# A row softmax whose tile context is closed behind the first six loads

## The chip, the cores and the metric

The kernel runs on one core of a Trainium2 chip. The metric is the device time of one execution in microseconds. A profile is one further execution, taken by the hardware profiler; its span runs from the first to the last instruction of the program, and the execution's device time is a little longer than that.

A core has several engines with instruction queues of their own: PE (matrix products, without arithmetic here), DVE (vector work), ACT (functions of one argument), POOL (a further vector engine) and SP, which only issues copies and waits. Sixteen copy engines, called DMA in the profile, move the data between device memory and on-chip memory.

## The reference

```python
def setup_inputs():
    batch, seq, dim = 16, 1024, 512
    return {
        "x": np.random.randn(batch, seq, dim).astype(np.float32),
    }

def reference(x: np.ndarray) -> np.ndarray:
    x_max = np.max(x, axis=-1, keepdims=True)
    exp_x = np.exp(x - x_max)
    return (exp_x / np.sum(exp_x, axis=-1, keepdims=True)).astype(np.float32)
```

A softmax over each of 16384 rows of 512 values: 33.55 MB in, 33.55 MB out, in float32.

## The kernel before

**Tiles and stages.** The rows are cut into 16 groups of 128 partitions by 8 rows (`GROUP`); one group is 128 x 4096 values, 2 MB. A load or a store moves two groups, 4 MB, so there are eight of each, called L0 to L7 and S0 to S7 here. The on-chip buffer `ring` holds 12 groups, that is six loads; everything is computed in place in it. L6 and L7 reuse the places of the first four groups, so they have to wait until S0 and S1 have read them out (`before` maps each late load to its store, `awaited` lists these stores).

**One group.** DVE takes the negated row maxima into `stat` (`rowmax`, line 146); ACT computes the exponential of each row with this as bias and leaves the row's sum in the same place (`exps`, line 135, a loop on ACT alone with eight row operations in an iteration); DVE inverts the sums into `recip` (line 160); and DVE or POOL multiplies the group by them (`scale`, line 162).

**What sets the order.** Three lists written by hand. `SEQUENCE` is the order of the work on DVE and POOL: M or MM is a maximum over one or two groups, D a scaling on DVE, P one on POOL. `ORDER` is the order of SP's late transfers. `AT_HEAD` says how many loads are lifted, after the program has been traced, out of the body's first block and put ahead of the barrier that opens the program (`loads_at_the_head`): one, on SP. The engines wait for each other through semaphores of the kernel's own: `loaded` for each load, `maxima`, `summed`, `inverted`, `scaled` for each store, and `stored` for the two stores that late loads wait for. The other stores raise `others`.

**What the tile context does.** The whole kernel is traced inside a tile context, a layer that finds dependences, adds its own semaphores and orders instructions. Six loads, a fence and the load of ACT's function table stand in a region with the order as written; `no_tile_sem_insts` lists the loads as copies that carry no semaphore of the context. All computation and the late transfers up to S6 stand in a critical section (line 186), which the context takes as one unit: on entry and on exit the engines of the section meet, here by way of PE. The last store, S7, follows the section, and behind it SP waits for `others` (line 207). On leaving the context (line 233, in the launch code) it adds an end of its own: a wait for what it tracks, a drain of every engine, a barrier, a clear of its semaphores by POOL, and a second barrier. Line 222 is the program's own opening, with a barrier too.

Of the kernel before, what the change touches and what calls it, by code (L numbers as in the profile page):

```python
# [8 lines left out]
EXP = mybir.ActivationFunctionType.Exp  # L9
AX = mybir.AxisListType.X  # L10
ACT, DVE, POOL, PE, SP = [
    getattr(mybir.EngineType, e) for e in ("Activation", "DVE", "Pool", "PE", "SP")
]
# [7 lines left out]
STORES = [2, 2, 2, 2, 2, 2, 2, 2]  # L21
# [1 line left out]
LOAD_AT = [sum(LOADS[:k]) for k in range(len(LOADS))]  # L23
STORE_AT = [sum(STORES[:k]) for k in range(len(STORES))]


ORDER = """
S0 S1 L6 L7 S2 S3 S4 S5 S6
"""


SEQUENCE = """
# [28 lines left out]
@with_exitstack  # L61
def kernel(
    ctx: ExitStack,
    tc: tile.TileContext,
    x: bass.AP,
    out: bass.AP,
):
    nc = tc.nc
    nc.at_finalize(loads_at_the_head)
    P = nc.NUM_PARTITIONS  # L70

    x_rows, out_rows = x.flatten_outer_dims(), out.flatten_outer_dims()
    d = x_rows.shape[1]
    assert x_rows.shape[0] == P * GROUPS * GROUP

    def sbuf(name, n):
        return ctx.enter_context(nc.sbuf_tensor(name, [P, n], F32))

    ring = sbuf("ring", RING * GROUP * d)

    stat = sbuf("stat", RING * GROUP)
    recip = sbuf("recip", RING * GROUP)

    def sem(name):
        return ctx.enter_context(nc.semaphore(name))

    maxima, summed, inverted = [sem(s) for s in ("maxima", "summed", "inverted")]
    loaded = [sem(f"loaded{k}") for k in range(len(LOADS))]
    scaled = [sem(f"scaled{k}") for k in range(len(STORES))]

    def load_of(g):
        return max(k for k in range(len(LOADS)) if LOAD_AT[k] <= g)

    def store_of(g):
        return max(k for k in range(len(STORES)) if STORE_AT[k] <= g)


    before = {
        k: store_of(LOAD_AT[k] + LOADS[k] - 1 - RING)
        for k in range(len(LOADS))  # L100
        if LOAD_AT[k] >= RING
    }

    awaited = sorted(set(before.values()))
    stored = {k: sem(f"stored{k}") for k in awaited}
    others = sem("others")

    def at(g):
        return g % RING

    def rows(g, groups=1):
        part = ring[:, at(g) * GROUP * d : (at(g) + groups) * GROUP * d]
        return part.rearrange("p (r d) -> p r d", d=d)

    def cols(t, g, groups=1):
        return t[:, at(g) * GROUP : (at(g) + groups) * GROUP]

    def in_dram(t, g, groups):
        k = load_of(g)
        assert load_of(g + groups - 1) == k  # L120
        part = t[P * GROUP * LOAD_AT[k] : P * GROUP * (LOAD_AT[k] + LOADS[k]), :]
        first = (g - LOAD_AT[k]) * GROUP
        part = part.rearrange("(p r) d -> p r d", p=P)
        return part[:, first : first + groups * GROUP, :]

    def load(k):
        g, n = LOAD_AT[k], LOADS[k]
        return nc.sync.dma_start(out=rows(g, n), in_=in_dram(x_rows, g, n))

    def store(k):  # L130
        g, n = STORE_AT[k], STORES[k]
        return nc.sync.dma_start(out=in_dram(out_rows, g, n), in_=rows(g, n))

    def exp(row, one):
        return nc.scalar.activation(  # L135
            out=row, in_=row, func=EXP, bias=one, scale=1.0, accum_out=one
        )

    def spread(t):
        return t.unsqueeze(2).to_broadcast([P, GROUP, d])  # L140


    def rowmax(g, groups):
        assert load_of(g) == load_of(g + groups - 1)
        nc.vector.wait_ge(loaded[load_of(g)], 16)  # L145
        nc.vector.reduce_max(  # L146
            out=cols(stat, g, groups), in_=rows(g, groups), axis=AX, negate=True
        ).then_inc(maxima, groups)

    def exps():  # L150
        with nc.Fori(0, GROUPS, 1, engines=(ACT,)) as g:
            nc.scalar.wait_ge(maxima, 1).then_inc(maxima, -1)  # L152
            row = nc.scalar.snap((g % RING) * GROUP)
            for r in range(GROUP):
                done = exp(ring[:, bass.ds((row + r) * d, d)], stat[:, bass.ds(row + r, 1)])
            done.then_inc(summed, 1)

    def scale(g, engine):
        nc.vector.wait_ge(summed, g + 1)
        nc.vector.reciprocal(out=cols(recip, g), in_=cols(stat, g)).then_inc(inverted, 1)  # L160
        engine.wait_ge(inverted, g + 1)
        engine.tensor_mul(  # L162
            out=rows(g), in0=rows(g), in1=spread(cols(recip, g))
        ).then_inc(scaled[store_of(g)], 1)

    def done_by(k):
        later = [a for a in awaited if a >= k]
        return stored[later[0]] if later else others

    def store_scaled(k):  # L170
        nc.sync.wait_ge(scaled[k], STORES[k])
        store(k).then_inc(done_by(k), 16)

    with tc.manual_schedule(engines={ACT, DVE, POOL, SP}):
        nc.scalar.preload_act_table(EXP)  # L175


        for k in range(min(before)):
            first = load(k).then_inc(loaded[k], 16)
            tc.info.no_tile_sem_insts.add(first.ins.name)  # L180
            tc.add_to_no_dep_group("loads", first.ins)
        tc.declare_fence(nc.sync.nop().ins, group="loads")

        pending = 16 * (len(STORES) - 2 - max(awaited))
        nc.scalar.nop().then_inc(others, pending)
        with tc.tile_critical(sync_engine=PE):
            nc.tensor.wait_ge(others, pending).then_inc(others, -pending)
            exps()
            for work in SEQUENCE.split():
                kind = work.rstrip("0123456789")  # L190
                g = int(work[len(kind) :])
                if kind in ("M", "MM"):
                    rowmax(g, len(kind))
                else:
                    scale(g, nc.vector if kind == "D" else nc.gpsimd)
            for transfer in ORDER.split():
                k = int(transfer[1:])
                if transfer[0] == "S":
                    store_scaled(k)
                else:  # L200
                    last = before[k]
                    since = max([a for a in awaited if a < last], default=-1)
                    nc.sync.wait_ge(stored[last], 16 * (last - since))
                    load(k).then_inc(loaded[k], 16)
            nc.sync.wait_ge(scaled[-1], STORES[-1])
        store(len(STORES) - 1)
        nc.sync.wait_ge(others, pending)


# [28 lines left out]
```

## Time and profile before

| what | value |
|---|---|
| device time, median of three runs | 161.18 us (160.99 to 161.60) |
| device time of the profiled execution | 161.16 us |
| span of the profiled execution | 159.4 us |
| copied | 33.55 MB read, 33.55 MB written |
| mean rate over the span | 421 GB/s |

The costliest groups of instructions; each row has line, engine and operation, what is written from what, and the number; then the busy time in us and the mean of one in ns; then the idle time of the engine just ahead of them and what ended it:

```profile
L135 ACT ACTIVATE ring<-ring,stat x128 | 90.4, 707 | 31.1 <-ACTq L152 31.1
L146 DVE TENSOR_REDUCE stat<-ring 128x16 f32<-128x8192 f32 (+1 forms) x10 | 69.5, 6956 | 15.5 <-DMA ring<-in_x_dram 15.5
L162 POOL TENSOR_TENSOR ring<-ring,recip 128x4096 f32<-128x4096 f32 x6 | 42.1, 7017 | 81.7 <-DVE recip L160 81.7
L162 DVE TENSOR_TENSOR ring<-ring,recip 128x4096 f32<-128x4096 f32 x10 | 51.1, 5110 | 0.3
```

An engine's letter with a q (SPq, POOLq) is its instruction queue: waits, drains, branches and issues of copies, which are not counted as busy.

### The profile page before, as it was taken

The page shows a single profiled execution, that of the slowest core. Times are in us where ns is not written, and L with a number is a line of the kernel's source. Part 1 is how long each engine was busy: PE and PEld are TensorE (multiplying, and loading weights), DVE is VectorE, ACT ScalarE, POOL GpSimd, SP SyncE. Part 2 cuts the span into 40 slices and gives each one's busy share as a digit, 9 for nine tenths or more (in the row PEclk, how much of TensorE's full clock was granted, in tenths as well). Part 3 has the DMA queues.
Part 4 walks back from the last instruction along what each step waited for, and adds up shares of the span by engine and source line. Part 5 has one row for each costly group of instructions (what it writes and reads, how often), then busy time and mean ns, then how long its engine had stood idle before and what let it go on. Part 6 is the DMA issues. An engine that isn't in the chain of part 4 may idle for free.

```text
span 159.4 us, 601 instructions
## 1 busy us (share of the span) xinstructions
DVE 121.8 (76%) x36; ACT 92.3 (58%) x257; POOL 42.3 (27%) x10
## 2 busy tenths in 40 slices
DVE  0009979999999999999999499999999999500000
ACT  3000799969307999999979990998699100000000
POOL 0000000000007904921960890098059100000000
DMA  7999999999999999999999999999999999999993
GB/s 263 444 469 403 428 469 419 395 469 452 395 428 477 411 395 395 395 493 428 395 436 477 403 395 493 428 395 469 436 411 411 477 428 395 477 428 411 436 461 156
DMA packets 2304, 67.11 MB, mean 421 GB/s; under 512 B 256, under 2 KB 256, under 8 KB 256
## 3 DMA queue, kind: packets, MB, share of 16 engines
q1 hardware_dynamic: 2304, 67.11, 98.4%
HBM read 33.55 MB, written 33.55 MB: 421 GB/s over the span
## 4 chain that ended last, share of the span: by engine, by line
DMA 45%; DVE 39%; issue 2%; DVEq 0%
DMA ring<-in_x_dram 25%; DVE ring L162 22%; DMA out_dram<-ring 20%; DVE stat L146 16%; DVE recip L160 1%; DVEq L145 0%
## 5 line engine op out<-in xcount | busy, mean ns | idle before, releaser
L135 ACT ACTIVATE ring<-ring,stat x128 | 90.4, 707 | 31.1 <-ACTq L152 31.1
L146 DVE TENSOR_REDUCE stat<-ring 128x16 f32<-128x8192 f32 (+1 forms) x10 | 69.5, 6956 | 15.5 <-DMA ring<-in_x_dram 15.5
L162 POOL TENSOR_TENSOR ring<-ring,recip 128x4096 f32<-128x4096 f32 x6 | 42.1, 7017 | 81.7 <-DVE recip L160 81.7
L162 DVE TENSOR_TENSOR ring<-ring,recip 128x4096 f32<-128x4096 f32 x10 | 51.1, 5110 | 0.3
L135 ACT ACTIVATION_READ_ACCUMULATOR ring<-ring,stat x128 | 23.8, 186 | 0.0
L160 DVE RECIPROCAL recip<-stat 128x8 f32<-128x8 f32 x16 | 3.0, 191 | 0.0
L175 ACT ACT_TABLE_LOAD x1 | 1.3, 1283 | 0.8 <-PEq L222 0.8
L222 POOL MEMSET const-float32-0.0<- 128x1 f32 x1 | 0.1, 98 | 0.2 <-issue 0.2
L222 POOL MEMSET const-bfloat16-1.0<- 128x1 bf16 x1 | 0.1, 103 | 0.0
L222 POOL MEMSET const-uint8-127<- 128x1 uint8 x1 | 0.1, 103 | 0.0
L222 POOL MEMSET const-float32-1.0<- 128x1 f32 x1 | 0.1, 99 | 0.0
## 6 DMA issues: line engine op xcount, KB each, us to landing
ring<-in_x_dram SPq DMA_DIRECT2D x8, 4096.0 KB, 25.9
out_dram<-ring SPq DMA_DIRECT2D x8, 4096.0 KB, 23.9
```

What stands on the lines that cost most here:

```text
L135: return nc.scalar.activation(out=row, in_=row, func=EXP, bias=one, scale=1.0, accum_out=one)
L146: nc.vector.reduce_max(out=cols(stat, g, groups), in_=rows(g, groups), axis=AX, negate=True).then_inc(maxima, groups)
L160: nc.vector.reciprocal(out=cols(recip, g), in_=cols(stat, g)).then_inc(inverted, 1)
L162: engine.tensor_mul(out=rows(g), in0=rows(g), in1=spread(cols(recip, g))).then_inc(scaled[store_of(g)], 1)
L175: nc.scalar.preload_act_table(EXP)
L222: nc = _bacc.Bacc("TRN2", target_bir_lowering=False, num_devices=1)
```

## The change

The context now holds only the first six loads. It is closed and compiled inside the kernel, and everything else is traced after that, outside any context. The group and the fence of the loads, the preset of `others` and the critical section are gone; the order as written is asked for SP alone, since only SP has instructions inside. S7 joins `ORDER` and raises `others` as the stores from S2 on do; SP's last wait counts six stores instead of five, and a nop follows it. The load of ACT's table follows the close. `SEQUENCE`, the late loads and their waits are the same. `tc.close()` ends the trace of the context and `tc.compile()` turns it into instructions, its end with drains, barriers and the clear among them; leaving the context in the launch code then adds nothing more.

```diff
 ORDER = """
-S0 S1 L6 L7 S2 S3 S4 S5 S6
+S0 S1 L6 L7 S2 S3 S4 S5 S6 S7
 """
...
-    with tc.manual_schedule(engines={ACT, DVE, POOL, SP}):
-        nc.scalar.preload_act_table(EXP)
...
+    with tc.manual_schedule(engines={SP}):
         for k in range(min(before)):
             first = load(k).then_inc(loaded[k], 16)
             tc.info.no_tile_sem_insts.add(first.ins.name)
-            tc.add_to_no_dep_group("loads", first.ins)
-        tc.declare_fence(nc.sync.nop().ins, group="loads")
-
-        pending = 16 * (len(STORES) - 2 - max(awaited))
-        nc.scalar.nop().then_inc(others, pending)
-        with tc.tile_critical(sync_engine=PE):
-            nc.tensor.wait_ge(others, pending).then_inc(others, -pending)
-            exps()
...
-            nc.sync.wait_ge(scaled[-1], STORES[-1])
-        store(len(STORES) - 1)
-        nc.sync.wait_ge(others, pending)
+    tc.close()
+    tc.compile()
+
+    nc.scalar.preload_act_table(EXP)
+    exps()
+    for work in SEQUENCE.split():
...
+    for transfer in ORDER.split():
+        k = int(transfer[1:])
+        if transfer[0] == "S":
+            store_scaled(k)
+        else:
+            last = before[k]
+            since = max([a for a in awaited if a < last], default=-1)
+            nc.sync.wait_ge(stored[last], 16 * (last - since))
+            load(k).then_inc(loaded[k], 16)
+    nc.sync.wait_ge(others, 16 * (len(STORES) - 1 - max(awaited)))
+    nc.sync.nop()
```

More of the change, by code (lines that the diff above doesn't have):

```diff
@@ L180 @@
             tc.info.no_tile_sem_insts.add(first.ins.name)
-            tc.add_to_no_dep_group("loads", first.ins)
-        tc.declare_fence(nc.sync.nop().ins, group="loads")
-        pending = 16 * (len(STORES) - 2 - max(awaited))
-        nc.scalar.nop().then_inc(others, pending)
-        with tc.tile_critical(sync_engine=PE):
-            nc.tensor.wait_ge(others, pending).then_inc(others, -pending)
-            exps()
[L189 to L204, printed above, removed]
-            nc.sync.wait_ge(scaled[-1], STORES[-1])
-        store(len(STORES) - 1)
-        nc.sync.wait_ge(others, pending)
+    tc.close()
[3 more added lines that the diff above has]
+    for work in SEQUENCE.split():
+        kind = work.rstrip("0123456789")
+        g = int(work[len(kind) :])
+        if kind in ("M", "MM"):
+            rowmax(g, len(kind))
+        else:
+            scale(g, nc.vector if kind == "D" else nc.gpsimd)
+    for transfer in ORDER.split():
+        k = int(transfer[1:])
+        if transfer[0] == "S":
+            store_scaled(k)
+        else:
+            last = before[k]
[4 more added lines that the diff above has]
+    nc.sync.nop()
 _INS = ['x']
```

## The prediction

> **What bounds the kernel now.** I read the page first, then the copy queues, the chain of waits, the rows of the opening and of the closing stage, and last the records of semaphore changes, which the trace keeps beside the rows that are printed.
>
> ```profile
> span 159.4 us, 601 instructions
> DVE 121.8 (76%) x36; ACT 92.3 (58%) x257; POOL 42.3 (27%) x10
> DMA  7999999999999999999999999999999999999993
> q1 hardware_dynamic: 2304, 67.11, 98.4%
> ```
>
> No engine fills the span, but the sixteen copy engines do: 98.4% of it, and nine tenths or more in every slice but the first and the last. 67.11 MB is the input once and the output once, so nothing can be left out of it. The chain of waits names DVE for 39%, yet that is only one of two parallel stories: the transfers stand back to back whatever DVE does. Landing times show it. The first load lands at 12.30 us, then 21.98, 31.70, 41.41, 51.12 and 61.35, then S0 at 71.09, S1 at 80.96, L6 at 90.45, L7 at 100.21, and at the end S6 at 148.90 and S7 at 158.57: always 9.5 to 10.2 us, the time of 4 MB. Work is queued well before its turn: S1 is issued at 61.75 against 71.09, S6 at 128.55 and S7 at 138.03 against 148.90. So compute has at least 9.3 us of slack. What can be won lies ahead of the first packet or behind the last.
>
> ```profile
> core 0: us, DVE busy (x) ACT busy (x) POOL busy (x), PEclk, DMA share, GB/s
> 149.00:157.30 8.30, 0.00 (x0) 0.00 (x0) 0.00 (x0) 1.00 0.98 422
> 157.30:158.60 1.30, 0.00 (x0) 0.00 (x0) 0.00 (x0) 1.00 0.01 0
> 158.60:159.40 0.80, 0.00 (x0) 0.00 (x0) 0.00 (x0) 1.00 0.00 0
> ```
>
> The table by stretches shows the end: data moves until 157.3, the completion marks arrive until 158.57, and then 0.8 us pass in which nothing is copied or computed. The rows of line 233 say what these are:
>
> ```profile
> L233 SPq DRAIN  x3: 7/7/7, 158.7 to 159.0; - x3
> L233 POOLq DRAIN  x2: 34/52/71, 158.9 to 159.1; - x2
> L233 POOLq EVENT_SEMAPHORE_RANGE_CLEAR  x1: 73/73/73, 159.0 to 159.0; - x1
> ```
>
> SP's wait for S7 runs from 158.59 to 158.62. Then come a drain on every engine, a barrier (over at about 158.93), POOL's clear of the context's semaphores at 159.01, and a second barrier that PE leaves last, at 159.378, the span's end. The durations are tens of nanoseconds; the hops between engines make the 0.76 us.
>
> **The change part by part.** *The end.* The context's closing moves from behind S7 to behind the first six loads. SP now ends with its wait for the six late stores and a nop. The wait ends at 158.62 as before; for the nop I allow 0.03 (the fence nop of before took 17 ns, and SP starts consecutive instructions about 0.06 apart). The program ends at 158.65 instead of 159.378: 0.73 us less of span.
>
> *Behind the span.* The profiled execution has 161.16 us, 1.78 more than its span. The semaphore records show what happens there: nine increments of semaphore 2 (159.611, .645, .852, .896, .919, 160.017, .057, .091, .138), then all semaphores cleared in five blocks up to 160.699, then nine more increments (160.924 to 161.281). Nine over five engines is a walk there and back. I read the order from the blocks: the lowest (up to 53) clears slowest, 7 ns each, and fits PE, whose semaphore rows take 51 ns against 17 to 21 elsewhere; the highest (207 to 255) starts first, 0.12 us after the fifth increment. That fits SP as the turning point. Before, all engines enter this walk together, PE's first increment is 0.233 after its last instruction, and the third hop, POOL's, takes 0.207 where the second walk needs 0.038: it was late by 0.17. After the change PE is done at about 4 us, POOL at about 124 and DVE at 137.7, so four hops have been walked long before, and only SP is late. Its own way from last instruction to increment isn't shown: at most 159.919 - 159.332 = 0.587, at least nothing, and PE's 0.233 is the nearest row; I take 0.23. The fifth increment then comes at 158.65 + 0.23 = 158.88 instead of 159.919, which is 1.04 us earlier, and all that follows it moves along. With 0.587 the gain is 0.68, with zero 1.27.
>
> The Trainium skill, "Runtime: NRT & Kernel Launch", section "The ~15µs preamble/postamble breakdown", gives such a walk as about 355 ns and lists the runtime's closing stages as fixed lengths added to a kernel. The second walk here agrees (161.281 - 160.924 = 0.357); the first takes 0.527. Taken as fixed lengths, the page speaks against any gain beyond the span, and the sum would be 160.43; by the records it is 160.12.
>
> *The opening.* Behind the sixth load's issue (over at 3.16) SP now passes a drain, two barriers and POOL's clear. The same steps took 0.76 at the end, so the close is over at about 4.0. A drain doesn't wait for copies that are under way: SP's took 7 ns at 137.84 with S5 and S6 queued, and 131 ns at 0.43 behind the first load. Nothing waits for SP then: its next issue is S0 at 39.92.
>
> ```profile
> 0.00 3.16 SPq L128 DMA_DIRECT2D ring<-in_x_dram  x6
> 0.79 1.28 ACT L175 ACT_TABLE_LOAD   x1 [0.79 <-PEq L222]
> 12.32 4.42 DVE L146 TENSOR_REDUCE stat<-ring 128x8 f32<-128x4096 f32 x1 [12.32 <-DMA ring<-in_x_dram]
> ```
>
> The table load moves from 0.79 to about 4.0 and ends near 5.3; ACT first needs it at 17.09. DVE's first reduction waits for the load until 12.32 in any case. Cover for all of this: 8.3 us. If that were gone, the price would still be nothing until 9.3 us more are lost.
>
> *The critical section.* The fence nop, ACT's preset of `others`, PE's wait, and the section's exit go. The exit held S7 from 137.69 to 138.03, so S7 is issued 0.34 earlier. S6 occupies the copy engines until 148.90, so this is worth nothing. SP's waits, the late loads and their order stay, on the same queue. The loads lose their group and fence; since they write different parts of the ring and carry no semaphore of the context, none is held behind another.
>
> *Sum.* 161.16 - 1.04 = 160.12 us. The profiled execution lies 0.02 below the median of the runs, 161.18, so this is 0.66% under that median.
>
> **The rivals.** *Only the program's own tail goes.* The runtime keeps its 1.78 us behind the program. For it: the walk can start with something that counts from the last engine's end, and SP's way into it may be as long as the bound of 0.587. Against it: POOL's late hop shows that the walk waits for arrivals. 161.16 - 0.73 = 160.43, which is 0.46% under the median.
>
> *The close waits for the six loads* (slower). A context that ends could wait for all that it issued. Place: the drain at 3.2 us, on every engine. For it: at the end of before, the context does wait for S7 (158.59). Against: that store carries the context's own semaphore 127; the six loads are excepted from these. Price: compute starts at 61.35 + 0.8 = 62.2 instead of 12.32. DVE needs 137.66 - 12.32 less 3.2 of later load waits, 122.1, so S7 is issued at 184.3; S6, 9.5 ahead, lands some 12.3 after its issue (as the first, unqueued load), at 187.1, and S7 9.67 later, at 196.8. With 1.55 behind it (161.16 - 158.57 - 1.04): 198.3 us. It decides as soon as the close ends later than 12.32 + 9.3 = 21.6 us; before that point it costs nothing.
>
> *The first load loses its place at the head.* It is lifted out of the body's first block, which the close ends early. If it isn't found there, it is issued where the second one was, at 0.79, and all copies slide by 0.79: 160.91, no change that can be told. Against it: the loads are still traced inside the context, in that block.
>
> **How the numbers follow.** The forecast (gain of more than the span's) has 0.66, the program's tail alone 0.23, the close that waits 0.04, the lost head 0.04, something unnamed that slows 0.03. About 0.5%, 0.8 us, is what a measurement of this kernel tells from no change, so the line is at 160.37. The forecast's bounds are 159.89 and 160.48; the runs of before scatter from 160.99 to 161.60, 0.2 below and 0.4 above their median. Range: 159.70 to 160.65, which takes in the tail-only case and leaves out less than 2 in 10. Faster: 0.87 of the forecast and 0.3 of the tail-only case, 0.64. Slower: the waiting close, the unnamed and a little of the lost head, 0.08. The same: 0.28.
>
> **What would show it.** A span of 158.6 to 158.7, with no drain or clear behind S7's landing and the clear of the context's semaphores near 4 us; the table load near 4 us; DVE's first reduction still at about 12.3; S7 issued near 137.7 and landing about 9.7 behind S6; and the fifth increment of semaphore 2 about 0.2 behind SP's last instruction. A remainder of about 1.78 behind the span would be the first rival. A first reduction behind 61 us would be the second. A first landing near 13.1 would be the third. A slower copy, a mean well under 421 GB/s, would overturn the whole sum, since nothing in it moves the copies.

## The result and the profile after

The changed kernel takes 160.05 us (median; 159.83 to 160.18) where the kernel before takes 161.38 beside it (160.99 to 162.05): a ratio of 0.9913, with a 95% interval of 0.9891 to 0.9935. That is 1.33 us less. The profiled execution has 160.08 us against 161.16.

The head of the page of the changed kernel, with the lines that answer to those of before:

```profile
span 158.8 us, 572 instructions
DVE 121.8 (77%) x36; ACT 92.2 (58%) x257; POOL 42.3 (27%) x10
DMA  7999999999999999999999999999999999999996
q1 hardware_dynamic: 2304, 67.11, 98.9%
```

The copies are the same, 67.11 MB in 2304 packets, and so is the engines' work. The span is shorter by 0.6 us, and 29 instructions are gone. What counts is at the two ends. The end first, by stretches (length, then busy time of the engines, clock, share of the copy engines, GB/s):

```profile
149.00:157.30 8.30, 0.00 (x0) 0.00 (x0) 0.00 (x0) 1.00 0.98 422
157.30:158.60 1.30, 0.00 (x0) 0.00 (x0) 0.00 (x0) 1.00 0.01 0
158.60:158.80 0.20, 0.00 (x0) 0.00 (x0) 0.00 (x0) 1.00 0.00 0
```

The first two rows are those of before; the third, 0.8 us long before, has shrunk to 0.2. SP's last wait is the last instruction of the program, and no other row of the end is left (line 200 is the nop; the wait of line 199 and the nop left this one row):

```profile
L200 SPq EVENT_SEMAPHORE  x1: 17/17/17, 158.7 to 158.7; - x1
```

The drains and barriers of the context's end now stand in the opening, under the line of `tc.close()`:

```profile
L179 POOLq EVENT_SEMAPHORE  x4: 17/17/17, 3.4 to 3.8; - x4
L179 SPq DRAIN  x3: 7/7/123, 3.2 to 3.7; - x3
L179 POOLq DRAIN  x2: 34/38/41, 0.7 to 3.6; - x2
```

They are over at 3.95, and the first reduction still waits for nothing but its load, as the opening in order of time shows:

```profile
0.00 3.17 SPq L127 DMA_DIRECT2D ring<-in_x_dram  x6
...
3.97 1.28 ACT L181 ACT_TABLE_LOAD   x1 [3.97 <-PEq L179]
12.37 4.42 DVE L145 TENSOR_REDUCE stat<-ring 128x8 f32<-128x4096 f32 x1 [12.37 <-DMA ring<-in_x_dram]
```

The trace's records of semaphore 2 show the rest. Times are in us from the span's start; "landing" is S7's last completion mark:

```
before   landing 158.574  159.611 159.645 159.852 159.896 159.919 160.017 160.057 160.091 160.138   ... 161.281
after    landing 158.730    4.184 124.456 124.914 137.959 158.890 158.934 158.972 159.007 159.055   ... 160.199
```

Nine increments belong to the runtime's first walk. Four of them now happen during the kernel: at 4.2 us, at 124.5, at 124.9 and at 138.0, each 0.1 to 0.5 us after the last instruction of PE, ACT, POOL and DVE (3.95, 124.34, 124.39 and 137.81). The records don't name the engine; e5 to e7 test this reading. Only SP's, the fifth, follows the landing, after 0.16 us instead of 1.35 (1.345).

So the profiled 1.08 us are made of three pieces. From landing to last instruction 0.03 instead of 0.80: 0.77 won. From last instruction to the end of the device time 1.32 (160.08 - 158.764) instead of 1.78 (161.16 - 159.378): 0.47 won. And S7 happened to land 0.16 later in this execution. Without that, the gain is 1.24, beside 1.33 between the medians.

### The profile page after: what moved, and what is told of

Its sections match the earlier page's. It is cut to its first block, busy times and chain, and to the rows that moved or that the text cites. A ratio compares the mean times of both kernels' runs of the same rounds, so it can differ in the third digit from the quotient of the medians.

```text
span 158.8 us, 572 instructions
## 1 busy us (share of the span) xinstructions
DVE 121.8 (77%) x36; ACT 92.2 (58%) x257; POOL 42.3 (27%) x10
## 2 busy tenths in 40 slices
DMA packets 2304, 67.11 MB, mean 423 GB/s; under 512 B 256, under 2 KB 256, under 8 KB 256
## 3 DMA queue, kind: packets, MB, share of 16 engines
q1 hardware_dynamic: 2304, 67.11, 98.9%
## 4 chain that ended last, share of the span: by engine, by line
DMA 45%; DVE 39%; issue 2%; DVEq 0%
DMA ring<-in_x_dram 26%; DVE ring L161 22%; DMA out_dram<-ring 20%; DVE stat L145 16%; DVE recip L159 1%; DVEq L144 0%
```

## The experiments

All but e4 are edits of the changed kernel. The records of semaphore 2 carry the verdicts that are smaller than a measurement's scatter; a table of them follows e7.

**e1, the changed kernel again**, without an edit, as the base for e2 and e3, and further on for e8 and e10.

> The changed kernel, unaltered, beside the others on one chip. Every theory: 0.99 of the kernel before (0.989 to 0.994), about 1.3 us faster. From S7's last completion mark to the last increment of semaphore 2 some 1.47 us, where the kernel before has 2.71.

Measured: 159.96 us against 161.28, ratio 0.9915 (0.9901 to 0.9928); 1.47 us from the landing to the last increment. The gain repeats.

**e2, all engines end together.** Four waits with a nop each, no drain, no barrier, no clear.

```diff
     nc.sync.wait_ge(others, 16 * (len(STORES) - 1 - max(awaited)))
     nc.sync.nop()
+    for late in (nc.tensor, nc.scalar, nc.gpsimd, nc.vector,):
+        late.wait_ge(others, 16 * (len(STORES) - 1 - max(awaited)))
+        late.nop()
```

> PE, ACT, POOL and DVE also wait for the six late stores, so that all five engines end together behind S7; no barrier, drain or clear is added. Theory (engines that end early have walked their part of the runtime's closing walk): POOL's own way into the walk, 0.53 us, is exposed again, so the time from S7's landing to the last increment grows by 0.45 to 0.50, to about 1.95, and the kernel takes some 160.5, 0.3% more than the changed one. Rival (only the program's own tail was saved): nothing changes, 1.47 and 160.05.

Measured: 160.51 us, ratio to before 0.9948 (0.9935 to 0.9962), 0.55 more than e1. The four waits are the only new rows, and they are over 0.08 us behind the landing:

```profile
L203 ACTq EVENT_SEMAPHORE  x1: 17/17/17, 158.8 to 158.8; - x1
L203 POOLq EVENT_SEMAPHORE  x1: 17/17/17, 158.8 to 158.8; - x1
L203 DVEq EVENT_SEMAPHORE  x1: 21/21/21, 158.8 to 158.8; - x1
L203 PEldq EVENT_SEMAPHORE  x1: 51/51/51, 158.8 to 158.8; - x1
```

The program's own end is only 0.05 us longer than in the changed kernel (0.08 for 0.03). What lies behind the span is 1.81 us (160.65 - 158.84) instead of 1.32, so 0.49 come back there. The rival by which only the program's tail was saved falls: about two fifths of the gain is the walk that four engines have already behind them. From the landing to the last increment it is 2.01 us, 0.54 more than in e1, where 0.45 to 0.50 was expected: the expectation left out that SP's increment is followed by the next after 0.097 us here, and after 0.044 in e1.

**e3, one barrier at the end.**

```diff
     nc.sync.nop()
+    nc.all_engine_barrier()
```

> One barrier over all engines behind the last wait, without the clear and the second barrier. Theory: the barrier's own 0.3 us and then the exposed walk, 0.45 to 0.5: 0.75 to 0.85 more from landing to the last increment than in the changed kernel, some 160.85. Rival (only the program's own tail was saved): 0.3 more, 160.35.

Measured: 160.75 us, ratio 0.9963 (0.9950 to 0.9977), 0.79 more than e1. The barrier's rows at the end:

```profile
L201 SPq DRAIN  x1: 7/7/7, 158.7 to 158.7; - x1
L201 SPq EVENT_SEMAPHORE  x1: 17/17/17, 158.9 to 158.9; - x1
...
L201 PEldq EVENT_SEMAPHORE  x1: 51/51/51, 158.9 to 158.9; - x1
```

The barrier is over 0.3 us behind the landing (158.66 to 158.96), and the rest of the 0.79 is the exposed walk again. By the records it is 0.74 from landing to last increment, just under the 0.75 to 0.85 expected. A barrier whose rows take 7 to 51 ns each costs more behind the program than in it.

**e4, the kernel before with S7 inside the critical section**, issued as soon as it is scaled.

```diff
 ORDER = """
-S0 S1 L6 L7 S2 S3 S4 S5 S6
+S0 S1 L6 L7 S2 S3 S4 S5 S6 S7
 """
...
-        pending = 16 * (len(STORES) - 2 - max(awaited))
+        pending = 16 * (len(STORES) - 1 - max(awaited))
...
-            nc.sync.wait_ge(scaled[-1], STORES[-1])
-        store(len(STORES) - 1)
         nc.sync.wait_ge(others, pending)
```

> The kernel before with S7 moved into the critical section, so that S7 is issued as soon as it is scaled, 0.34 us earlier, and the section ends behind it. Theory: S7 queues behind S6 in any case, its landing doesn't move, and the time is that of before within 0.3%. Rival (the gain came from the section's exit in front of S7): 0.3 to 1.3 us faster, ratio 0.992 to 0.998.

Measured: 161.44 us against 161.28, ratio 1.0012 (1.0003 to 1.0021). S7 was issued 0.30 earlier, at 137.74, and landed at 158.61 (158.57 before): the earlier issue is worth nothing. The kernel is even a little slower, and SP's rows at the end say why:

```profile
L231 SPq EVENT_SEMAPHORE  x4: 17/22/28, 158.8 to 159.6; - x4
L231 SPq DRAIN  x3: 7/7/7, 158.9 to 159.2; - x3
L231 SPq COMPARE_BRANCH  x1: 33/33/33, 158.6 to 158.6; - x1
```

In the kernel before, SP's branch out of the section and two of its waits ran at 148.9 to 149.2, behind S6 and under S7's flight:

```profile
L233 SPq EVENT_SEMAPHORE  x2: 17/22/28, 149.1 to 149.1; - x2
L233 SPq COMPARE_BRANCH  x1: 33/33/33, 148.9 to 148.9; - x1
```

In e4 they stand behind S7, and the fifth increment comes 1.58 us after the landing instead of 1.35.

**e5, e6, e7: one engine late beside SP**, to read the walk's order.

```diff
     nc.sync.nop()
+    for late in (nc.tensor,):
+        late.wait_ge(others, 16 * (len(STORES) - 1 - max(awaited)))
+        late.nop()
```

(`nc.gpsimd` in e6, `nc.vector` in e7.)

> Beside SP, PE alone waits for the six late stores. Theory (a walk PE, ACT, POOL, DVE, SP and back, each hop waiting for its engine): PE's increment comes 0.235 after its last instruction and four hops of 0.14 in all follow; fifth increment 0.45 behind S7's landing, 0.29 more than in the changed kernel (0.16). Rival (any late engine costs the same, since the stage starts when the last engine ends): 0.65, as with all four late.

> Beside SP, POOL alone waits for the six late stores. Theory: POOL's own way of 0.54 us and two hops of 0.07: fifth increment 0.64 behind S7's landing, all of what four late engines cost. Rival (the cost is shared by the engines, or is PE's place at the head of the walk): well under 0.5.

> Beside SP, DVE alone waits for the six late stores. Theory: DVE's own way is 0.15 us (137.81 to 137.96 in the changed kernel) and one hop of 0.02 follows: fifth increment 0.22 behind S7's landing, 0.06 more than in the changed kernel. Rival (any late engine costs the same): 0.65.

Measured, one execution each for e5 to e7, from S7's landing, in us:

```
kernel                      fifth increment   last increment   device time
before                           1.345            2.707          161.16
after                            0.160            1.469          160.08
e2, four engines late            0.645            2.007          160.65
e5, PE late                      0.459            1.821          160.45
e6, POOL late                    0.645            2.010          160.60
e7, DVE late                     0.218            1.580          160.25
e3, barrier                      0.845            2.210          160.75
```

All three fifth increments came out as the walk PE, ACT, POOL, DVE, SP says, to about 0.01 us. In e6 the records read 4.210 for PE and 124.610 for ACT, then POOL's at 159.289, 0.54 us after its last wait, DVE's 0.044 behind it and SP's 0.023 behind that. POOL alone costs what all four cost, because its way into the walk is the longest; PE's 0.24 and DVE's 0.15 hide under it. ACT was not made late alone.

**e8, no load at the head** (`AT_HEAD = {}`), which makes the third rival's condition true.

> The changed kernel with no load lifted to the head. Theory: the first load is issued at 0.79 instead of 0.00, all copies slide by 0.79, the first landing comes at 13.1, and the kernel takes 160.8, the gain over the kernel before shrinks to 0.5 us. Rival (the copies' start is covered elsewhere): 160.0.

Measured: 160.68 us against 161.30, ratio 0.9960 (0.9939 to 0.9981). The first load's issue moves to 0.74, and the first landing to 13.02 (12.34 in the changed kernel):

```profile
0.74 2.95 SPq L127 DMA_DIRECT2D ring<-in_x_dram  x6
...
13.04 4.42 DVE L145 TENSOR_REDUCE stat<-ring 128x8 f32<-128x4096 f32 x1 [13.04 <-DMA ring<-in_x_dram]
```

0.72 more than e1, for 0.74 of delay: the start of the copies is paid in full, within the runs' scatter. The change alone didn't lose it.

**e9, the context closed ahead of the loads.** The first load is still lifted to the head; the other five are issued outside the context. For that `loads_at_the_head` searches all blocks of the program, not shown here.

```diff
-    with tc.manual_schedule(engines={SP}):
-        for k in range(min(before)):
-            first = load(k).then_inc(loaded[k], 16)
-            tc.info.no_tile_sem_insts.add(first.ins.name)
     tc.close()
     tc.compile()
+    for k in range(min(before)):
+        load(k).then_inc(loaded[k], 16)
```

> The context is closed empty, ahead of all loads; the first load is still lifted to the head, and the other five follow outside the context. An empty context seems to add no drain and no barrier, so these leave the opening. Theory: they were covered by the first load's flight until 12.3 us, and the time is that of the changed kernel within 0.2%. Rival (the barriers behind the loads cost what they cost at the end): 0.7 us faster, 159.3.

Measured: 159.99 us against 161.30, ratio 0.9918 (0.9904 to 0.9932), as the changed kernel. The expectation's side remark was wrong: an empty context does end with its drains and barriers, in SP's queue from 0.78 to 1.38, so that the second load is issued at 1.44 instead of 0.79. So the barriers have not left the opening, and the equal time alone doesn't decide against the rival. It shows that half a microsecond and more of barriers in front of five loads costs no more than behind them, under the first load, whose completion marks begin at 11.8 us. What decides is a comparison with the kernel before, which has no such barriers in the opening: the first load lands at 12.34 in the changed kernel and at 12.30 before, S0 at 71.07 and 71.09. The barriers moved no copy, so the rival by which they cost in the opening what they cost at the end falls.

**e10 and e11, the close held back** until the second and until the sixth load has landed.

```diff
+        nc.sync.wait_ge(loaded[1], 16)
     tc.close()
```

(`loaded[5]` in e11.)

> Ahead of the close SP waits for the second load, so that all engines are held until 22.0 + 0.7 us. Theory (9.3 us of slack from the first reduction at 12.3): reductions of the second load start 9.6 late, S1 is issued at 71.3 instead of 61.8, just behind S0's landing at 71.1, the copy queue runs dry for 1.3 to 2.1 us, and the kernel takes 161.3 to 162.1. Rival (a late start is paid in full): 10 us more, 170. Rival (there is more slack than read): 160.0.

Measured: 163.02 us against 161.30, ratio 1.0106 (1.0090 to 1.0122), 3.06 more than e1 and 0.9 above the expected 161.3 to 162.1. By stretches, around S1's issue:

```profile
68.00:70.00 2.00, 2.00 (x1) 2.00 (x7) 0.00 (x0) 1.00 0.83 360
70.00:71.00 1.00, 1.00 (x1) 1.00 (x5) 0.00 (x0) 1.00 0.01 0
71.00:72.00 1.00, 1.00 (x3) 1.00 (x4) 0.69 (x1) 1.00 0.39 164
```

S1 was issued at 71.14, S0 had landed at 71.02, so S1 had used up its 9.3 us of slack, about as worked out (71.3). The copy engines stood still together from 70.69 to 71.98, 1.3 us, or 1.6 us for each on average, as expected: a transfer's packets end ahead of its marks, and S1's first packet came 0.84 behind its issue. The queue thus has to be refilled about 1.2 us before the landing, and by this estimate the slack that costs nothing is nearer 8.1; no run delayed the start by less.

The other 1.4 us of the loss arose with the engines busy. S1 landed 2.1 us later than in e1, L6 2.5, L7 3.1 and S7 still 3.1. So the loss grew up to L7's end and not behind it. Two stretches show it, around S1's end and around L7's end, the two places behind the gap where the copies change direction. The engines were about as busy as in e1 and moved less; the first two rows are e10's, the last two e1's:

```profile
80.00:82.00 2.00, 2.00 (x1) 2.00 (x7) 0.00 (x0) 1.00 0.94 262
98.00:104.00 6.00, 6.00 (x1) 6.00 (x19) 6.00 (x1) 1.00 1.00 366
80.00:82.00 2.00, 2.00 (x1) 2.00 (x7) 2.00 (x1) 1.00 1.03 442
98.00:104.00 6.00, 5.97 (x5) 4.38 (x13) 0.00 (x0) 1.00 1.02 431
```

S1, with L6 issued 0.4 us behind it, took 12.1 us from its issue to its landing; S0 of e11, which ran alone, took 11.1. Why the engines were slower then stays open.

> Ahead of the close SP waits for the sixth load: the second rival of the prediction, made on purpose. Theory: first reduction at 62.1, S7 issued at 184.2, landing at 196.8, 198.3 us in all. If the copies can't be kept busy as worked out there, the time differs by more than 3 us.

Measured: 201.95 us in one run, 3.65 more than expected. The copy engines in 40 slices:

```profile
DMA  8999999999980000039400999999899999999997
GB/s 314 418 444 444 457 431 418 418 418 444 444 366 0 0 0 0 0 157 470 209 0 0 418 418 418 418 418 418 366 438 451 418 418 418 431 451 451 444 418 314
```

There are two gaps: 28.7 us before S0 and another 11.9 us between S0 and S1. From S1's issue at 109.99 nine transfers, S1, L6, L7 and S2 to S7, follow each other and end at 200.60, 10.1 us each; S7, issued at 183.56, is again last in a queue.

## Why the prediction was right, and where it was off

**The sum**: 160.12 us was forecast, and 160.05 was measured, inside the range. The time was hit more closely than the gain: 1.04 us was forecast, and 1.24 shows in the profiles once the later landing is taken out (1.33 between the medians). Scatter hid the rest, and that is luck: in the profiled execution S7 landed 0.16 later, and in the runs the kernel before took 161.38, not 161.18. The later landing also put the span, 158.76, just above the 158.6 to 158.7 named as a sign.

**What bounds the kernel**: right. The copy engines' share is 98.9% instead of 98.4%, and all of the gain lies behind their last packet. The slack of compute, 9.3 us, was read from landings; by e10's gap about 8.1 of it are free (9.3 less 1.2), so a close that waits would begin to cost some 1.2 us earlier than the 21.6 named.

**The end**: right, mis-sized by little. The term was 0.73; it measures 0.77, since the nop for which 0.03 was allowed has no row of its own, and SP's one row ends 0.03 behind the landing.

**Behind the span**: the mechanism was right, as e2 and e5 to e7 show; the size was too small. The prediction took 1.04 in all, so 0.31 here, and 0.47 was measured. SP's way into the walk was taken from PE's row, 0.23, and is 0.13. And the walk back was taken as unchanged, 0.22, but takes 0.165: SP's increment to DVE's is 0.044 instead of 0.098. This shorter hop shows only where DVE's own increment lies far back; in e2, e3 and e5 to e7, where it came 0.023 before SP's, the hop took 0.097 or 0.098 again. Both errors point the same way. The later landing hid them in the profiled execution (160.08 for 160.12).

**The Trainium skill's table of the runtime's stages** ("Runtime: NRT & Kernel Launch", "The ~15µs preamble/postamble breakdown") puts a time on each stage; that these are fixed was the prediction's reading. The page's 355 ns, given there for the walk of the opening barrier, fits the second walk here: 0.357 us in the profiles of both kernels. The first walk has no fixed length in these runs: from the last instruction to the ninth increment it is 0.76 us before and 0.29 after, and what it adds behind the program goes by which engine is late.

**The opening**: right in cost. The close is over at 3.95 for 4.0 predicted, the table load starts at 3.97, the first reduction at 12.37. The clear of the context's semaphores, named with the change and predicted near 4 us, doesn't exist: the rows of line 179 have none. The landings, which didn't move, bear out the cover.

**The critical section's exit**: right. S7 issued earlier lands no earlier (e4). That its waits are themselves a cost when they stand behind S7 wasn't seen.

**The first rival**, only the program's own tail: refuted by e2. **The second**, a close that waits: it doesn't. Its worked-out price of 198.3 was wrong by 3.65 us. The step that failed is "S6, 9.5 ahead, lands some 12.3 after its issue (as the first, unqueued load)": it took the queue behind the gap for empty and overlooked the second gap, whereas nine transfers are queued from S1 on. **The third**, the lost head: it wasn't lost; its price of 0.79 measures 0.72.

## What to carry to other kernels

Where copies fill the span, as here, look at what stands between the last landing and the end of the device time, and take everything from there that doesn't wait for that landing: a context's end, its drains, barriers and branches cost nothing under a load's flight and 0.77 us here behind a store's. Let every engine but the one that waits for the last store run out of instructions early; a common barrier at the end costs its own 0.3 us and 0.5 us more behind the program. A transfer at the end of a full queue gained nothing from being issued earlier (e4), but the first transfer's issue counted one to one (e8).

## What was not expected of the hardware

In all thirteen profiles of this study, both kernels' and the experiments', the device time is the last increment of semaphore 2 less 0.117 to 0.126 us. So the records show where each tenth of a microsecond behind the span goes, and a single profile tells apart what the scatter of whole runs (159.86 to 160.03 for e1) hardly does.

The engines' ways from their last wait to their first increment differ: POOL 0.54 us (e6), PE 0.24 (e5), DVE 0.15 (e7), SP 0.13 (the changed kernel). ACT's was not measured behind a wait of its own. Why POOL's is so long stays open.

A drain didn't wait for copies under way: SP's behind six queued loads took 123 ns (line 179), and the later ones 7 ns, with the first load landing only at 12.3 us.
